# Turning the normalised memory by DMA instead of by TensorE

## The chip, the cores and the metric

The kernel runs on one core of a Trainium2 chip. The metric is the device time of one execution in microseconds (us). Below, PE is TensorE's matmul, PEld its weight load, DVE VectorE, ACT ScalarE, POOL GpSimd and SP SyncE, which issues the DMAs.

## The reference

Two layers work on `x` (512 tokens of 1024 numbers, float32). Each layer is a half-step SwiGLU block, a mixing block with three branches (stick-breaking attention, forgetting attention, attention over a memory), and another half-step SwiGLU block, each with an RMS norm before and after. What matters here is the memory branch: 256 memory rows, normalised once, give keys and values in both layers.

```python
def _rmsnorm(t, g):
    t32 = t.astype(jnp.float32)
    t32 = t32 * lax.rsqrt(jnp.mean(t32 * t32, axis=-1, keepdims=True) + RMS_EPS)
    return t32.astype(t.dtype) * g
...
    mem_n = _rmsnorm(mem, mem_norm_g)
...
        k_mem, v_mem = jnp.split(mem_n @ w_mem_kv[l], 2, axis=-1)
        o_mem = _memory_attention(_split_heads(q_mem, N_MEM_HEADS), _split_heads(k_mem, N_MEM_HEADS),
                                  _split_heads(v_mem, N_MEM_HEADS))
```

## The kernel before

**Products.** Every float32 product is made of three matmuls (`mm3`, lines 212 to 214): each operand is split into a high part and a low part, `h = round(v)` by ACT (line 182) and `l = v - h` by DVE (line 183), and `h*h`, `h*l` and `l*h` are summed in PSUM. A matmul contracts over the 128 partitions, so an operand must lie with the contracted dimension on the partitions.

**Queue.** The work is written as a list of jobs (`Queue`); a job has weight units and a generator that traces its matmuls. A `Unit` is loaded by SP into a raw buffer (`fetch`, line 256), split into `wh` and `wl` (four buffers each), and its raw buffer then takes the next unit. The planner that turns the trace into programs orders each engine's instructions ahead of the run, by the order in which they were traced and by when it reckons them ready; at run time every engine follows its own program and waits on semaphores. Tiles with one tag share a fixed number of buffers: "v" has six, "rs" one, "tri" two, "raw" two.

**Around the change.** The first feed-forward block of a layer ends in `down`: 144 matmuls of 128 x 512 in eight groups (`pda`), with three weight units for each of three passes. Between the first pass and the rest stands the job `mem_norm` (given as `aside`); in layer 0 the small vectors are turned (`vectors`) just ahead. As tokens finish, the chain of `Sub` (residual, norm, eight transposes `uta`, split into `us_a`) runs for the next block on ACT and DVE. After `down` come the jobs of `mem_kv`: `keys` (matmuls `pmk`, 128 x 256), `values` (`pmv`, 128 x 512), which contract over the 1024 numbers of a memory row and read `mn`, the memory turned so that those numbers lie on partitions. Then `q_mem` begins the mixing block, which needs all of `us_a`.

**`mem_norm` before.** Per layer it loads the two 128-row tiles of the memory (`mraw`, line 1062), multiplies each row with its own factor (`mem_rstd`, DVE, line 1063), and turns them with 16 transposes of 128 x 128 on PE (`mt`, line 1070), four to a PSUM bank. The norm's weight now runs along partitions, so ACT multiplies it in as a per-partition scale while it makes the high part (line 1075), and DVE makes the low part from the same bank (line 1076): eight of each per layer, 128 x 256. The weight itself, `memg`, is turned by PE in `vectors` (lines 122, 126, 128).

**A pattern that is there already.** A DMA transposes 16-bit words. The attention's stick heads and the feed-forward's hidden tiles turn 32-bit words by it: ACT copies the words so that all upper and all lower halves lie together (`turn_out`, line 1152; line 814), SP issues a transposing DMA (`turn_over`, line 1161; line 815), and ACT copies the halves back into words (line 1237; line 822).

Of the kernel before, what the change touches and what calls it, by code (L numbers as in the profile page):

```python
# [9 lines left out]
F32 = mybir.dt.float32  # L10
F32R = mybir.dt.float32r
BF16 = mybir.dt.bfloat16
U16 = mybir.dt.uint16
AF = mybir.ActivationFunctionType
ALU = mybir.AluOpType
# [3 lines left out]
P = 128  # L19
# [4 lines left out]
def kernel(  # L24
# [38 lines left out]
    nc = tc.nc  # L63
    _, S, D = x.shape
    M = mem.shape[1]
    L = w_in.shape[0]
    NT = S // P
    ND = D // P
    MT = M // P
# [12 lines left out]
    cst = ctx.enter_context(tc.tile_pool(name="cst", bufs=1))  # L82
# [6 lines left out]
    ident = cst.tile([P, P], F32, name="ident")  # L89
# [9 lines left out]
    def tmp(name):  # L99
        return sb.tile([P, S], F32, tag="f32t", bufs=8, name=name)  # L100
# [3 lines left out]
    def stile(shape, tag, name, dt=F32R):  # L104
        return sb.tile(shape, dt, tag=tag, bufs=BUFS[tag], name=name)
# [4 lines left out]
    def pbank(tag, name):  # L110
        return ps.tile([P, S], F32, tag=tag, bufs=4, name=name)

    gain_srcs = (ffn1_pre_g, ffn1_post_g, mix_pre_g, mix_post_g, ffn2_pre_g, ffn2_post_g)

    memg = cst.tile([P, ND], F32, name="memg")
    nbgate = cst.tile([P, L, 3 * ND], F32, name="nbgate")
    bgate = cst.tile([P, L, 3 * ND], F32, name="bgate")
    bfor = cst.tile([NH, L], F32, name="bfor")

    def vectors():  # L120
        vecs, n = tmp("vecs"), L * 3 * ND
        nc.gpsimd.dma_start(vecs[0:ND, 0:P], mem_norm_g.rearrange("(d p) -> d p", p=P))
        nc.gpsimd.dma_start(vecs[0:n, P:2 * P], b_gate.rearrange("l (d p) -> (l d) p", p=P))
        yield 0.0
        pt = pbank("z", "vecs_t")
        nc.tensor.transpose(pt[:, 0:ND], vecs[0:ND, 0:P], ident[0:ND, 0:ND])
        nc.tensor.transpose(pt[:, P:P + n], vecs[0:n, P:2 * P], ident[0:n, 0:n])
        nc.scalar.copy(memg[:], pt[:, 0:ND])
        nc.scalar.copy(bgate[:].rearrange("p l d -> p (l d)"), pt[:, P:P + n])
        nc.scalar.mul(nbgate[:].rearrange("p l d -> p (l d)"), pt[:, P:P + n], -1.0)  # L130
        yield 0.2
# [47 lines left out]
    def split(h_ap, l_ap, src, scale=None, later=False):  # L179

        if scale is None:
            both = [nc.scalar.copy(h_ap, src)]  # L182
            make = lambda: nc.vector.tensor_tensor(l_ap, src, h_ap.bitcast(F32), ALU.subtract)  # L183
        else:
            both = [nc.scalar.activation(h_ap, src, AF.Copy, scale=scale)]  # L185
            make = lambda: nc.vector.scalar_tensor_tensor(l_ap, src, scale, h_ap.bitcast(F32), ALU.mult, ALU.subtract)  # L186
        if later:
            return make
        both.append(make())
        if Q.pinned:  # L190
            for ins in both:
                tc.keep_in_program_order(ins)
        return both
# [292 lines left out]
    def rstd(st, a, b=None, beside=None):  # L486

        s, m, y, w = st[:, a:a + 1], st[:, 3:4], st[:, 4:5], st[:, 5:6]
        if b is None:
            nc.scalar.activation(y, s, AF.Ln, bias=eps_t[:])  # L490
            nc.vector.tensor_scalar(m, s, D * EPS, None, ALU.add)
        else:
            nc.vector.tensor_scalar(m, s, st[:, b:b + 1], D * EPS, ALU.add, ALU.add)
            nc.scalar.activation(y, m, AF.Ln)
            if beside is not None:
                beside()
        nc.scalar.activation(y, y, AF.Exp, scale=-0.5)

        nc.vector.scalar_tensor_tensor(w, m, y, y, ALU.mult, ALU.mult)
        nc.vector.scalar_tensor_tensor(y, w, -3.0, y, ALU.add, ALU.mult)  # L500
        return y

    class Sub:

# [61 lines left out]
        def residual(self, t):  # L566

            r = rstd(self.sf[t], 0, 1, self.held[t])
            f, h = self.fs[t], hT[t]
            if self.g_pre is None:  # L570
                for c in HF if t < NT - 1 else (HF[1], slice(0, S // 2), slice(S // 2, S)):
                    nc.vector.scalar_tensor_tensor(h[:, c], f[:, c], r, h[:, c], ALU.mult, ALU.add)
                    nc.sync.dma_start(out[0, t * P:(t + 1) * P, c], h[:, c])
            else:
                nc.vector.scalar_tensor_tensor(h[:], f[:], r, h[:], ALU.mult, ALU.add)
                self.squared(h[:], self.sh[t], 0, f[:])

        def normed(self, t, parts=(FULL_D,)):

            r = rstd(self.sh[t], 0)  # L580
            for c in parts:
                nc.vector.scalar_tensor_tensor(self.fs[t][:, c], hT[t][:, c], r, self.gq[:, c], ALU.mult, ALU.mult)
# [34 lines left out]
    def ffn(l, src, wg, wu, wd, dst, name, spare, parked, plan, aside=None):  # L617
# [348 lines left out]
        if name == "a0":  # L966
            Q.add([], vectors)
# [69 lines left out]
    mem_rstd = cst.tile([P, MT, 2], F32, name="mem_rstd")  # L1037
# [10 lines left out]
    def mem_norm(l, mn):  # L1048

        mn[:] = [stile([P, ND, M], "tri", f"mn{l}_{i}") for i in range(2)]  # L1050
        raws = []
        if l == 0:
            ms, r = mem_rstd[:, :, 0], mem_rstd[:, :, 1]
            for out_, in_, f, s in ((r, ms, AF.Ln, 1.0), (r, r, AF.Exp, -0.5)):
                tc.keep_in_program_order(nc.scalar.activation(out_, in_, f, scale=s))
            nc.vector.tensor_tensor(ms, ms, r, ALU.mult)
            nc.vector.tensor_tensor(ms, ms, r, ALU.mult)
            nc.vector.tensor_scalar(ms, ms, -0.5, 1.5, ALU.mult, ALU.add)
            nc.vector.tensor_tensor(r, r, ms, ALU.mult)
        for t in range(MT):  # L1060
            raw = stile([P, D], "v", f"mraw{l}_{t}", F32)
            nc.sync.dma_start(raw[:], mem[0, t * P:(t + 1) * P, :])
            nc.vector.tensor_scalar(raw[:], raw[:], mem_rstd[:, t, 1:2], None, ALU.mult)
            raws.append(raw)
        yield 0.0
        for i in range(ND // 2):
            pt = pbank("z", f"mt{l}_{i}")
            for j in range(2):
                for t in range(MT):
                    nc.tensor.transpose(pt[:, j * M + t * P:j * M + (t + 1) * P],  # L1070
                                        raws[t][:, (2 * i + j) * P:(2 * i + j + 1) * P], ident[:])
            for j in range(2):
                d = 2 * i + j
                src = pt[:, j * M:(j + 1) * M]
                nc.scalar.activation(mn[0][:, d], src, AF.Copy, scale=memg[:, d:d + 1])
                nc.vector.scalar_tensor_tensor(mn[1][:, d], src, memg[:, d:d + 1],
                                               mn[0][:, d].bitcast(F32), ALU.mult, ALU.subtract)
            yield 0.45

    def mem_kv(l, mn, ks, vs):  # L1080

# [551 lines left out]
    def begin():  # L1633
# [31 lines left out]
        def stats(t):  # L1665
            sub.squared(hT[t][:], sub.sh[t], 0, sub.fs[t][:])
            return rstd(sub.sh[t], 0)
# [59 lines left out]
    for l in LAYERS:  # L1727
        i, mn = 3 * l, []
        ma = ffn(l, subs[i], ffn1_w_gate, ffn1_w_up, ffn1_w_down, subs[i + 1], f"a{l}", "v",
                 park[2 * l] if l else None, PLAN, lambda l=l, mn=mn: mem_norm(l, mn))  # L1730
        rest = mem_kv(l, mn, *kvs[l])
        mb = mixing(l, subs[i + 1], *kvs[l], rest, subs[i + 2])
        if l == 0:
            Q.weave(begin(), ma["first"])
        else:
            for part, units in zip(mc["next"], (ma["early"][:2], ma["early"][2:])):
                part.extend(units)
            for un in ma["early"][2:]:
                un.place = "v"
            boundary(mc, mc["end"], ma["first"])  # L1740
        boundary(ma, ma["end"], mb["first"])
        mb["run"]()
        mc = ffn(l, subs[i + 2], ffn2_w_gate, ffn2_w_up, ffn2_w_down, subs[i + 3], f"c{l}", "o", park[2 * l + 1], PLAN)
        for part, units in zip(mb["next"], (mc["early"][:2], mc["early"][2:])):
                part.extend(units)
        boundary(mb, mb["end"], mc["first"])
# [25 lines left out]
```

## Time and profile before

| | us |
|---|---|
| median of 3 runs | 2338.09 |
| lowest, highest | 2337.59, 2340.59 |
| the profiled execution | 2342.67 |
| its span | 2340.9 |
| mean clock granted to PE | 0.999 |

The profile is of one execution. Its page lists each engine's busy time and share of the span. A line of the timeline gives start and duration in us, the engine, the line of the kernel, the operation, the tile written and those read, shapes and count, and in brackets how long the engine was idle before it and what released it. Matmuls overlap: the time that one takes from the engine is the distance between starts. A line of a tile's view gives a count, the shortest, median and longest duration in ns, the first and last start, and the shapes. A line of the windows view gives the stretch, its length, and the busy time and count of PE, PEld, DVE, ACT and POOL in it, then PE's clock, the DMA share and GB/s.

### The profile page before, as it was taken

How to read it: one execution, taken by the hardware profiler on the slowest of the kernel's cores; microseconds unless marked ns; L12 is line 12 of the kernel's file. 1: busy time of each engine (PE TensorE's matmuls, PEld its weight loads, DVE VectorE, ACT ScalarE, POOL GpSimd, SP SyncE). 2: the span in 40 equal slices, each digit the busy share in tenths (PEclk: the TensorE clock that was granted, in tenths of full speed). 3: DMA queues.
4: the chain of work that ended last, by engine and by line, in shares of the span. 5: the costliest groups of instructions: out<-in, count | busy, mean ns of one | idle time of the engine just before them, and what ended most of it. 6: DMA issues, size and time to landing. Idle time of an engine off the chain costs nothing.

```text
span 2340.9 us, 30650 instructions
## 1 busy us (share of the span) xinstructions
PE 2322.9 (99%) x11463; PEld 1960.2 (84%) x11463; DVE 1764.2 (75%) x2253; ACT 1509.8 (64%) x2216; POOL 81.2 (3%) x182
## 2 busy tenths in 40 slices
PE   9999999999999999999999999999999999999998
PEld 7888888888888888888898888888888888888887
DVE  8877877566777688878798788765677767887785
ACT  6677465577756556775656774655787674667744
POOL 0000000000111000000000000000001100000000
PEclk9999999999999999999999999999999999999999
DMA  6667454344423555674646665544444236466744
GB/s 207 190 176 221 146 189 141 93 115 114 122 73 105 187 186 164 185 199 152 226 144 186 196 185 179 185 114 95 119 105 116 81 118 200 160 195 176 220 138 144
DMA packets 340344, 365.44 MB, mean 156 GB/s; under 512 B 120778, under 2 KB 231650, under 8 KB 340196
## 3 DMA queue, kind: packets, MB, share of 16 engines
q1 hardware_dynamic: 340100, 363.46, 52.0%
q8 instruction: 90, 1.47, 0.3%
q14 instruction: 58, 0.48, 0.1%
q0 software_dynamic: 96, 0.03, 0.0%
HBM read 319.39 MB, written 16.78 MB: 144 GB/s over the span
## 4 chain that ended last, share of the span: by engine, by line
PE 85%; DMA 5%; ACT 4%; DVE 3%; issue 2%; DVEq 0%; SPq 0%; ACTq 0%
PE pg L213 4%; PE pg L212 4%; PE pg L214 4%; PE pda L213 3%; PE pda L212 3%; PE pda L214 3%; PE pdc L213 3%; PE pdc L212 3%; PE pdc L214 3%; PE pb L213 1%; PE pb L212 1%; PE pb L214 1%; PE pq L213 1%; PE pq L212 1%; PE pq L214 1%
## 5 line engine op out<-in xcount | busy, mean ns | idle before, releaser
L212 PE MATMUL pg<-us_a,wh_wg 128*128 128x512 f32 x384 | 150.4, 392 | 0.0
L213 PE MATMUL pg<-us_a,wh_wg 128*128 128x512 f32 x384 | 149.7, 390 | 0.0
L214 PE MATMUL pg<-us_a,wl_wg 128*128 128x512 f32 x384 | 149.6, 390 | 0.0
L183 DVE TENSOR_TENSOR wl_da<-raw_da,wh_da 128x1024 fp32r<-128x1024 f32 x50 | 60.8, 1223 | 44.6 <-ACT wh_da L182 44.4
L183 DVE TENSOR_TENSOR wl_dc<-raw_dc,wh_dc 128x1024 fp32r<-128x1024 f32 x50 | 61.0, 1223 | 44.1 <-ACT wh_dc L182 44.1
L213 PE MATMUL pdc<-wl_dc,ahc 128*128 128x512 f32 x224 | 87.7, 392 | 0.0
L213 PE MATMUL pda<-wl_da,aha 128*128 128x512 f32 x224 | 87.6, 391 | 0.0
L214 PE MATMUL pdc<-wh_dc,alc 128*128 128x512 f32 x224 | 87.2, 389 | 0.0
L214 PE MATMUL pda<-wh_da,ala 128*128 128x512 f32 x224 | 87.2, 389 | 0.0
L212 PE MATMUL pdc<-wh_dc,ahc 128*128 128x512 f32 x224 | 86.6, 390 | 0.5 <-ACT pdc L895 0.5
L212 PE MATMUL pda<-wh_da,aha 128*128 128x512 f32 x224 | 86.5, 389 | 0.0
L186 DVE SCALAR_TENSOR_TENSOR wl_wg<-raw_wg,wh_wg 128x1024 fp32r<-128x1024 f32 x48 | 58.7, 1223 | 35.8 <-ACT wh_wg L185 35.6
L214 PEld LDWEIGHTS pg<-us_a,wl_wg 128*128 128x128 f32 x384 | 72.1, 188 | 15.1
L212 PEld LDWEIGHTS pg<-us_a,wh_wg 128*128 128x128 f32 x384 | 72.1, 188 | 14.2
L213 PEld LDWEIGHTS pg<-us_a,wh_wg 128*128 128x128 f32 x384 | 72.1, 188 | 14.2
L182 ACT CAST wh_da<-raw_da 128x1024 fp32r<-128x1024 f32 x50 | 52.1, 1050 | 46.9 <-PE pda L214 19.4
L182 ACT CAST wh_dc<-raw_dc 128x1024 fp32r<-128x1024 f32 x50 | 52.3, 1049 | 46.0 <-DMA raw_dc<-in_ffn_w_down_dram 13.9
L182 ACT CAST wh_uc<-raw_uc 128x1024 fp32r<-128x1024 f32 x44 | 46.4, 1054 | 34.5 <-PE pwc1g L214 7.7
L182 ACT CAST wh_ua<-raw_ua 128x1024 fp32r<-128x1024 f32 x44 | 46.2, 1052 | 30.2 <-PE pwa0g L214 7.6
L183 DVE TENSOR_TENSOR wl_uc<-raw_uc,wh_uc 128x1024 fp32r<-128x1024 f32 x44 | 53.7, 1220 | 14.5 <-ACT wh_uc L182 14.5
L183 DVE TENSOR_TENSOR wl_gc<-raw_gc,wh_gc 128x1024 fp32r<-128x1024 f32 x40 | 48.5, 1221 | 20.3 <-ACT wh_gc L182 20.3
L1237 ACT COPY pws<-ts 128x1024 uint16<-128x1024 uint16 (+1 forms) x64 | 55.4, 914 | 12.2 <-DMA ts<-ns 11.9
(643 smaller groups left out, 7921.1 us busy)
## 6 DMA issues: line engine op xcount, KB each, us to landing
raw_da<-in_ffn_w_down_dram SPq DMA_DIRECT2D x66, 512.0 KB, 5.3
raw_dc<-in_ffn_w_down_dram SPq DMA_DIRECT2D x66, 512.0 KB, 4.6
raw_ga<-in_ffn_w_gate_dram SPq DMA_DIRECT2D x52, 512.0 KB, 4.7
raw_ua<-in_ffn_w_up_dram SPq DMA_DIRECT2D x52, 512.0 KB, 4.5
raw_gc<-in_ffn_w_gate_dram SPq DMA_DIRECT2D x52, 512.0 KB, 4.1
raw_uc<-in_ffn_w_up_dram SPq DMA_DIRECT2D x52, 512.0 KB, 4.4
raw_wg<-in_w_gate_dram SPq DMA_DIRECT2D x48, 512.0 KB, 3.6
raw_wo<-in_w_out_dram SPq DMA_DIRECT2D x24, 512.0 KB, 3.7
```

Of the source, the lines that this page charges most:

```text
L182: both = [nc.scalar.copy(h_ap, src)]
L183: make = lambda: nc.vector.tensor_tensor(l_ap, src, h_ap.bitcast(F32), ALU.subtract)
L186: make = lambda: nc.vector.scalar_tensor_tensor(l_ap, src, scale, h_ap.bitcast(F32), ALU.mult, ALU.subtract)
L212: nc.tensor.matmul(pt, lh, rh, start=start, stop=False, skip_group_check=free)
L213: nc.tensor.matmul(pt, lh, rl, start=False, stop=False, skip_group_check=free)
L214: nc.tensor.matmul(pt, ll, rh, start=False, stop=stop, skip_group_check=free)
L1237: nc.scalar.copy(block_words(word, i), over[:, :, c:c + i + 1])
```

## The change

The 16 PE transposes per layer go, with the eight high and eight low parts that read them from PSUM, and the turned weight `memg`. Instead the weight is loaded as a row into all 128 partitions (`grow`, tag "rs", once per layer), and DVE multiplies a tile by its rows' factors and by that row in one operation. Then `flip_out` has ACT copy the tile's halves apart into a second "v" tile and SP issue one transposing DMA of all 2048 half-words per partition back into the first; `flip_back` has ACT put the words together, and `split` makes one high and one low part of 128 x 1024 per tile.

```diff
-    memg = cst.tile([P, ND], F32, name="memg")
...
-        nc.gpsimd.dma_start(vecs[0:ND, 0:P], mem_norm_g.rearrange("(d p) -> d p", p=P))
...
-        nc.tensor.transpose(pt[:, 0:ND], vecs[0:ND, 0:P], ident[0:ND, 0:ND])
...
-        nc.scalar.copy(memg[:], pt[:, 0:ND])
...
+    def flip_out(words, halves):
+
+        nc.scalar.copy(halves.bitcast(U16).rearrange("p (h k) -> p h k", h=2), words.bitcast(U16).rearrange("p (k h) -> p h k", h=2))
+        nc.sync.dma_start_transpose(words.bitcast(U16).rearrange("p (r q) -> p r q", q=P), halves.bitcast(U16))
+
+    def flip_back(words, over):
+
+        nc.scalar.copy(words.bitcast(U16).rearrange("p (k h) -> p h k", h=2), over.bitcast(U16).rearrange("p (h k) -> p h k", h=2))
...
     def mem_norm(l, mn):
 
         mn[:] = [stile([P, ND, M], "tri", f"mn{l}_{i}") for i in range(2)]
-        raws = []
+        raws, grow = [], stile([P, D], "rs", f"mg{l}", F32)
+        nc.sync.dma_start(grow[:], mem_norm_g.rearrange("(a d) -> a d", a=1).broadcast_to([P, D]))
...
-            nc.vector.tensor_scalar(raw[:], raw[:], mem_rstd[:, t, 1:2], None, ALU.mult)
+            nc.vector.scalar_tensor_tensor(raw[:], raw[:], mem_rstd[:, t, 1:2], grow[:], ALU.mult, ALU.mult)
             raws.append(raw)
         yield 0.0
-        for i in range(ND // 2):
-            pt = pbank("z", f"mt{l}_{i}")
-            for j in range(2):
-                for t in range(MT):
-                    nc.tensor.transpose(pt[:, j * M + t * P:j * M + (t + 1) * P],
-                                        raws[t][:, (2 * i + j) * P:(2 * i + j + 1) * P], ident[:])
-            for j in range(2):
-                d = 2 * i + j
-                src = pt[:, j * M:(j + 1) * M]
-                nc.scalar.activation(mn[0][:, d], src, AF.Copy, scale=memg[:, d:d + 1])
-                nc.vector.scalar_tensor_tensor(mn[1][:, d], src, memg[:, d:d + 1],
-                                               mn[0][:, d].bitcast(F32), ALU.mult, ALU.subtract)
-            yield 0.45
+        turned = []
+        for t, raw in enumerate(raws):
+            halves = stile([P, D], "v", f"mh{l}_{t}", F32)
+            flip_out(raw[:], halves[:])
+            turned.append(halves)
+            yield 0.0
+        for t, (raw, halves) in enumerate(zip(raws, turned)):
+            flip_back(halves[:], raw[:])
+            c = slice(t * P, (t + 1) * P)
+            split(mn[0][:, :, c], mn[1][:, :, c], halves[:].rearrange("p (d q) -> p d q", q=P))
+            yield 0.0
```

## The prediction

> **What bounds the kernel.** I read the page's busy times first, then the windows view of the two stretches that the change touches, then the timeline of PE inside them.
>
> ```profile
> PE 2322.9 (99%) x11463; PEld 1960.2 (84%) x11463; DVE 1764.2 (75%) x2253; ACT 1509.8 (64%) x2216; POOL 81.2 (3%) x182
> ```
> ```profile
> 326.10:348.65 22.55, 22.01 (x110) 18.21 (x109) 20.85 (x40) 17.00 (x42) 0.00 (x0) 1.00 0.22 84
> 1481.60:1509.48 27.88, 27.50 (x133) 22.79 (x134) 23.77 (x42) 19.11 (x45) 0.00 (x0) 1.00 0.32 113
> ```
>
> PE is idle for 18 us of 2340.9, so whatever leaves PE comes off the end, and whatever makes PE wait is added to it. The two windows run from the first scaling of a memory tile to the first key matmul that reads `mn`, once per layer; the columns are length, then busy us of PE, PEld, DVE, ACT and POOL, PE's clock, DMA share and GB/s. DVE (20.85 of 22.55) and ACT (17.00 of 22.55) have little room in layer 0, more in layer 1. So the question is what PE gains, and whether ACT and DVE still deliver in time.
>
> **What leaves PE.** Layer 0, then layer 1, in PE's timeline (start, duration, instruction):
>
> ```profile
> 325.97 0.39 PE L212 MATMUL pda<-wh_da,hida 128*128 128x512 f32 x1
> 326.88 2.19 PE L1070 MATMUL mt<-ident,mraw 128*128 128x128 f32 x16 [0.53 <-DVE mraw L1063]
> 328.83 0.48 PE L213 MATMUL pda<-wl_da,hida 128*128 128x512 f32 x1
> 329.14 0.40 PE L214 MATMUL pda<-wh_da,hida 128*128 128x512 f32 x1
> ```
> ```profile
> 1480.95 0.39 PE L214 MATMUL pda<-wh_da,hida 128*128 128x512 f32 x1
> 1481.61 0.66 PE L1070 MATMUL mt<-ident,mraw 128*128 128x128 f32 x4 [0.28 <-DVE mraw L1063]
> 1482.02 0.47 PE L212 MATMUL pda<-wh_da,hida 128*128 128x512 f32 x1
> ...
> 1484.87 0.39 PE L212 MATMUL pda<-wh_da,hida 128*128 128x512 f32 x1
> ...
> 1486.23 0.39 PE L212 MATMUL pda<-wh_da,hida 128*128 128x512 f32 x1
> 1486.99 1.53 PE L1070 MATMUL mt<-ident,mraw 128*128 128x128 f32 x12 [0.37 <-DVE mraw L1063]
> 1488.27 0.47 PE L213 MATMUL pda<-wl_da,hida 128*128 128x512 f32 x1
> ```
>
> Matmuls overlap, so I count starts, not durations. Undisturbed they start every 1.36/6 = 0.227 us (1484.87 to 1486.23 is six). Layer 0: 328.83 - 325.97 - 0.227 = 2.63, and the next start comes 0.31 behind instead of 0.227: with 0.03 for the starts after it, 2.74 us go. Layer 1: (1.07 - 0.227) + (2.04 - 0.227) = 2.65, and about 0.1 for each restart: 2.86.
>
> The transpose of `mem_norm_g` goes too; its neighbour for the gate's bias stays:
>
> ```profile
> 311.89 0.22 PE L126 MATMUL vecs_t<-ident,vecs 8*128 8x8 f32 x1
> 312.05 0.26 PE L127 MATMUL vecs_t<-ident,vecs 48*128 48x48 f32 x1
> ```
>
> That is 0.16 us from start to start. All of it: 2.74 + 2.86 + 0.16 = **5.76 us, the most that the change can bring**.
>
> **What ACT and DVE get.** The same kind of copies and transposes exist in the stick heads (`turn_out`, `turn_over`), which gives their prices; the rows are count, ns min/median/max, first and last start, forms.
>
> ```profile
> L1237 ACT COPY pws<-ts x64: 467/910/1370, 446.6 to 1781.4; 128x1024 uint16<-128x1024 uint16 x16, 128x768 uint16<-128x768 uint16 x16, 128x512 uint16<-128x512 uint16 x16, 128x256 uint16<-128x256 uint16 x16
> ...
> L1152 ACT COPY ns<-ts x48: 812/833/1065, 440.6 to 1775.7; 128x768 uint16<-128x768 uint16 x32, 128x1024 uint16<-128x1024 uint16 x16
> L1161 SPq DMA_TRANSPOSE ts<-ns x48: 1209/1232/2306, 441.9 to 1776.6; - x48
> ```
> ```profile
> L1075 ACT ACTIVATE mn<-mt,memg x16: 465/482/509, 328.1 to 1491.4; 128x256 fp32r<-128x256 f32 x16
> L1076 DVE SCALAR_TENSOR_TENSOR mn<-mt,memg,mn x16: 473/476/485, 328.6 to 1492.9; 128x256 fp32r<-128x256 f32 x16
> ```
> ```profile
> L1063 DVE TENSOR_SCALAR mraw<-mraw,mem_rstd x4: 745/747/752, 326.1 to 1486.2; 128x1024 f32<-128x1024 f32 x4
> ```
> ```profile
> L582 DVE SCALAR_TENSOR_TENSOR fa<-hfa,nha,gqa x8: 1276/1278/1285, 339.4 to 1521.6; 128x1024 f32<-128x1024 f32 x8
> ```
> ```profile
> L182 ACT CAST wh_mk<-raw_mk x8: 1032/1054/1057, 340.0 to 1514.3; 128x1024 fp32r<-128x1024 f32 x8
> L183 DVE TENSOR_TENSOR wl_mk<-raw_mk,wh_mk x8: 1215/1218/1226, 341.2 to 1516.5; 128x1024 fp32r<-128x1024 f32 x8
> ```
>
> `flip_back` writes 2048 half-words with a stride: the L1237 copy grows from 0.47 us (256) to 1.37 (1024), 0.30 per 256, so 1.37 + 4 x 0.30 = 2.57. `flip_out` reads with a stride: L1152 grows by about 0.22 from 768 to 1024, 1.05 + 4 x 0.22 = 1.93. Per layer ACT gets two of each and two casts of 1.05, 11.1 us, and loses eight of 0.48, 3.86: **+7.2 us**. DVE: each scaling grows from 0.75 to 1.28 (the form of L582), the eight 0.476 become two of 1.22: 1.06 - 1.37 = -0.3 us.
>
> Layer 0: the window shrinks to 22.55 - 2.74 = 19.8 us, in which ACT would have 17.00 + 7.2 = 24.2 us of work and DVE 20.5. ACT is **4.4 us over**, DVE 0.7. Layer 1: 26.3 us for ACT in 25.0, 1.3 over. In the other direction nothing is won: PE has no idle time left to lose.
>
> What absorbs the lateness is the lead that ACT and DVE have over PE. The tightest in layer 0 is the second key-weight unit:
>
> ```profile
> 346.97 2.35 DVE L183 TENSOR_TENSOR wl_mk<-raw_mk,wh_mk 128x1024 fp32r<-128x1024 f32 x2
> ```
> ```profile
> L212 PE MATMUL pmk<-mn,wh_mk x64: 278/283/365, 348.6 to 1521.6; 128*128 128x256 f32 x64
> ```
> ```profile
> L212 PE MATMUL pmk<-mn,wh_mk x32: 278/283/365, 1509.5 to 1521.6; 128*128 128x256 f32 x32
> ```
>
> (The key matmuls begin at 348.6 in layer 0 and 1509.5 in layer 1.) Its low part is there at 346.97 + 1.18 = 348.15. PE wants it 14 half-width matmuls after the first, at about half the pitch of 0.227 (an estimate from the rows above): 350.2. Its cast can start only when PE leaves an earlier unit's buffer, so it moves with PE and keeps 2.1 us of lead. I take 4.4 - 2.1 = **2.3 us of PE waiting in layer 0**, bounds 0 (the late work is all from the residual chains, which nobody needs yet) and 4.4 (none is covered). Layer 1: 1.3 is under the lead there, 0; upper bound 1.3.
>
> [...]
>
> **When PE comes early.** In layer 1 the third unit of `down`'s second weight set is bound by its load:
>
> ```profile
> 1482.22 2.00 ACT L182 CAST wh_da<-raw_da 128x1024 fp32r<-128x1024 f32 x2 [0.83 <-DVE fa L549]
> ```
> ```profile
> 1480.81 0.75 DVE L1063 TENSOR_SCALAR mraw<-mraw,mem_rstd 128x1024 f32<-128x1024 f32 x1
> 1481.47 0.68 DVE L549 SCALAR_TENSOR_TENSOR fa<-pda,gpa 128x512 f32<-128x512 f32 x1
> 1483.31 2.36 DVE L183 TENSOR_TENSOR wl_da<-raw_da,wh_da 128x1024 fp32r<-128x1024 f32 x2 [1.15 <-ACT wh_da L182]
> ```
>
> Its low part is done at 1483.31 + 1.18 = 1484.49 and PE wants it one matmul after 1484.87, 1485.10. Without the first four transposes PE is there 0.94 earlier, 1484.16: 0.3 us of wait.
>
> **What else is issued.** SP gets four transposes and two loads of the weight row. The transposes are twice the size of L1161's, so I take 2 x 1.23 = 2.46 us of issue each, and for landing
>
> ```profile
> DMA to landing us min/median/max: 3.0/3.5/8.1
> ```
>
> (the 64 transposes of 256 KB in the feed-forward part, line 815) 2.46 + (3.5 - 1.23) = 4.7 us, between 3.0 and 16.2 (twice 8.1). Behind their waits on SP stand loads of key weights and saves of `h`, none wanted before 340; DMA is busy 22% and 32% in these windows. Layer 0: scaling 326.1 to 327.4, `flip_out` to 329.3 and 331.2, second transpose issued at 331.8, landed 336.5 (the first 334.0; between 331.2 and then ACT has the residual chain, and what is queued behind a `flip_back` that still waits are weight casts, squares and copies into PE's banks), `flip_back`, cast and low part 2.57 + 1.05 + 1.22 = 4.84 more: `mn` is whole at 341.3, wanted at 348.6 - 2.9 = 345.7. The weight row takes the "rs" buffer when the last turned plane leaves it:
>
> ```profile
> L1222 DVE TENSOR_TENSOR_SCAN ns<-ns,cut x48: 921/955/1539, 437.4 to 1773.6; 128x383 f32<-128x383 f32 x32, 128x511 f32<-128x511 f32 x16
> ...
> L1194 POOL MEMSET cut<- x2: 634/636/637, 206.4 to 1369.1; 128x640 f32 x2
> ```
>
> `cut` took it at 206.4; now the weight row does and `cut` waits until 329, still 100 us before its first reader. A wait for that buffer on SP would hold weight loads: 0, at most 1 us. The "v" buffers (six) hold three weight units, two raw tiles and now two turned ones; the seventh is free once the pair at 1483.31 ends, ahead of the second `flip_out`: 0. The four PSUM banks that `mt` leaves had no one waiting.
>
> **Sum**: -5.76 + 2.3 + 0.3 = -3.2 us. The profiled execution took 2342.7 (span 2340.9 and 1.8 around it), 4.6 over the median 2338.09; -3.2 makes 2339.5 of it and **2334.9** of the median. About 0.2% (4.7 us) is what a measurement of this kernel can tell from no change.
>
> **Rivals.**
> 1. *ACT's lead covers everything.* Only the 0.3 stays: 2332.6. For it: much of what ACT does there is squares and residual chains. Against it: ACT and DVE both over.
> 2. *`flip_out` gets in front of that cast in layer 1.* Its input is ready at 1480.81 + 1.28 = 1482.1, the cast starts at 1482.22. Then the low part is late by 1.93 more: 2336.8. The order is fixed ahead of the run, and the cast was traced first, so it is the less likely.
> 3. *The expected gain is eaten by the weight pipeline*: all of ACT's 4.4 and 1.3 reach PE: -5.76 + 5.7 + 0.3, 2338.3.
> 4. *The transposes land late, slower than before.* ACT stands at `flip_back`, and weight casts behind it. With landing time L, `mn` is whole at 336.6 + L in layer 0 (decides from L = 9.1) and at 1487.5 + 1.93 + L + 4.84 = 1494.3 + L in layer 1 (PE there at 1509.5 - 2.9; L = 12.3). At L = 16.2 PE waits 7.1 + 3.9 = 11.0: +5.2, 2343.3. Against it: 3.5 is the median and DMA is quiet.
> 5. *PE's clock drops after such a wait.* If all of ACT's 4.4 us reach PE in one piece in layer 0 and PE then runs as long at half its clock, 4.4 us of matmuls cost 4.4 more: -5.76 + 8.8 + 0.3, 2341.4. Against it: the windows show the clock at 1.00; but the longest idle time in them is 0.53 us, so they cannot show it. [...]
>
> **Chances.** Forecast 0.44, its own range 2333.0 to 2337.0; rival 1 0.22; 2 0.09; 3 0.11; 4 0.10; 5 0.04. Faster by over 0.2% (under 2333.4): rival 1 and a fifth of the forecast, 0.31. Slower by over 0.2%: rival 4 and a little of 3 and 5, 0.12. Within: 0.57. The range goes from rival 1, less 1 us of scatter, to between rivals 3 and 4: 2331.5 to 2341.5.
>
> **What would show it.** PE rows with `mt` gone and `pda` starts 0.227 apart through 326 to 329; `flip_back` near 2.6 us, transposes landing near 4.7; a PE wait of about 2 us near 344 to 352 for `wl_mk` or `mn`, next to none at 1505 to 1520. Wrong would be: no such wait (rival 1), one of over 5 us (rival 4), or PE waits far from both windows, which nothing here foresees.

## The result, and the profile after

| | us |
|---|---|
| before, median of 6 runs | 2338.50 (2337.39 to 2341.13) |
| after, median of 6 runs | 2346.05 (2344.57 to 2348.77) |
| ratio, 95% interval | 1.0033 (1.0020 to 1.0046) |
| profiled execution before: span | 2340.9 |
| profiled execution after: span | 2344.3 |

The changed kernel is slower by 7.6 us (4.7 to 10.8 by the interval). The forecast of 2334.9 and its range to 2341.5 were wrong. The two profiled executions lie only 3.4 us apart, because the one shown of before lies 4 us above the median of its kind.

The page of the changed kernel gives the busy times:

```profile
PE 2321.8 (99%) x11430; PEld 1957.7 (84%) x11430; DVE 1762.4 (75%) x2241; ACT 1521.2 (65%) x2211; POOL 78.6 (3%) x181
```

PE has 33 instructions less on record and is still busy for nearly as long; ACT has gained 11.4 us. The view of PE's waits (line and tile that waited, who ended it, then total us, times and the longest) says where the loss is:

```profile
PE pmk L208 <- DVE nha L496: 4.8, 1, 4.8
PE pda L208 <- ACT pda L849: 2.2, 1, 2.2
...
PE uta L597 <- DVE fa L587: 0.6, 1, 0.6
```

Before, no wait of PE exceeded 1.2 us. The first and the third are in layer 0, the second in layer 1. (Lines of the changed kernel stand a few off those before: `mm3` is 208 to 210, `split`'s cast and low part 178 and 179, the square of a result 549, its scaling 554, the copy into a bank 849.)

PE's timeline around the first:

```profile
339.89 0.39 PE L210 MATMUL pda<-wh_da,hida 128*128 128x512 f32 x1
345.10 0.55 PE L208 MATMUL pmk<-mn,wh_mk 128*128 128x256 f32 x1 [4.82 <-DVE nha L496]
...
346.31 0.41 PE L210 MATMUL pmk<-mn,wl_mk 128*128 128x256 f32 x1
346.52 0.63 PE L208 MATMUL pda<-wh_da,hida 128*128 128x512 f32 x1
346.94 0.63 PE L209 MATMUL pda<-wl_da,hida 128*128 128x512 f32 x1
```

Until 339.89 `pda` matmuls start 0.227 apart. After the wait the key matmuls (`pmk`), half as wide, start 0.21 apart (0.12 before) and the `pda` matmuls 0.43: PE runs at half its clock (0.50 from 342.79 to 349.62, in the last section). That this is the clock, and not a late operand, is seen in the windows (columns as in the prediction; the clock is the third number from the end):

```profile
326.08:340.00 13.92, 13.92 (x63) 11.44 (x61) 7.67 (x11) 13.55 (x14) 1.17 (x3) 1.00 0.50 113
340.00:345.00 5.00, 0.28 (x2) 0.00 (x0) 4.75 (x10) 5.00 (x14) 0.00 (x0) 0.78 0.35 105
345.00:350.00 5.00, 4.90 (x15) 4.19 (x16) 4.20 (x10) 2.40 (x8) 0.00 (x0) 0.54 0.26 105
```

While PE stands still, ACT is busy for 5.00 of 5.00 us; DVE, idle for much of the time before, for 4.75. What PE waits for is not `mn`: that is whole at 342.6 (below). It is a bank of PSUM, the memory in which PE's sums stand. The releasers that the profile names are no operands of the key matmul: `nha L496` on DVE is a 128x1 factor that comes right behind a scaling of line 554 and ends within 0.1 us of it, and the weight load of the same matmul had waited 5.2 us for the square of line 549 on ACT. A finished group of `pda` keeps its bank until ACT has squared it (line 549) and DVE has scaled it (line 554), and ACT then copies the old sums into a free bank (line 849) before PE can start the next group. ACT's timeline:

```profile
332.48 2.53 ACT L506 COPY mh<-mraw 128x2048 uint16<-128x2048 uint16 x1 [0.37 <-DMA mraw<-mh]
...
336.76 2.52 ACT L506 COPY mh<-mraw 128x2048 uint16<-128x2048 uint16 x1
339.14 1.04 ACT L178 CAST wh_mk<-raw_mk 128x1024 fp32r<-128x1024 f32 x1
340.09 1.04 ACT L178 CAST mn<-mh 128x1024 fp32r<-128x1024 f32 x1
...
342.17 0.57 ACT L549 ACTIVATE sqa<-pda 128x512 f32<-128x512 f32 x1
...
345.31 0.58 ACT L849 COPY pda<-fa 128x512 f32<-128x512 f32 x1
```

and DVE's, where the scaling stands behind work that had waited for ACT:

```profile
341.36 1.22 DVE L179 TENSOR_TENSOR mn<-mh,mn 128x1024 fp32r<-128x1024 f32 x1
...
344.27 0.68 DVE L554 SCALAR_TENSOR_TENSOR fa<-pda,gpa 128x512 f32<-128x512 f32 x1
```

Read backwards: PE starts at 345.10, behind the scaling that ends at 344.95. In DVE's order that scaling stood behind low parts and residual work, the first of which had waited 1.91 us for a cast on ACT, until 340.22. The bank needs the square of the same group too (by the order of the groups, the one at 342.17). In ACT's order it stood behind both `flip_back`, two casts of `mn`, two weight casts and the square of a residual. The copy into the bank of the last group was issued at 345.31. In the kernel before, the same two stood at

```profile
335.50 0.58 ACT L844 COPY pda<-fa 128x512 f32<-128x512 f32 x1
...
339.40 0.58 ACT L544 ACTIVATE sqa<-pda 128x512 f32<-128x512 f32 x1
```

The copy is now 9.8 us later and the square 2.8, although PE ends the third late group 3.6 us earlier than before (339.89 against 343.45).

Layer 1 has the same chain, shorter; there the first `flip_back` also kept ACT idle for 1.10 us until its transpose had landed. ACT's timeline:

```profile
1500.12 2.53 ACT L506 COPY mh<-mraw 128x2048 uint16<-128x2048 uint16 x1
...
1505.34 0.61 ACT L549 ACTIVATE sqa<-pda 128x512 f32<-128x512 f32 x1
...
1507.84 0.59 ACT L849 COPY pda<-fa 128x512 f32<-128x512 f32 x1
```

and PE's, which goes on when that copy is done:

```profile
1505.90 0.39 PE L210 MATMUL pda<-wh_da,hida 128*128 128x512 f32 x1
1508.48 0.50 PE L208 MATMUL pda<-wh_da,hida 128*128 128x512 f32 x1 [2.19 <-ACT pda L849]
```

The new operations themselves, in the view of the tile `mh` (count, ns min/median/max, first and last start):

```profile
L501 ACT COPY mh<-mraw x4: 1889/1900/1902, 326.1 to 1490.6; 128x2048 uint16<-128x2048 uint16 x4
L502 SPq DMA_TRANSPOSE mraw<-mh x4: 1526/1858/2502, 328.0 to 1492.5; - x4
L506 ACT COPY mh<-mraw x4: 2515/2523/2527, 332.5 to 1500.1; 128x2048 uint16<-128x2048 uint16 x4
...
DMA to landing us min/median/max: 4.4/4.8/5.2
```

So each piece costs what was forecast (1.93, 2.57 and 4.7 us); what they displace was not seen.

**Theory A:** the regrouping copies and casts fill ACT, and what frees the PSUM banks stands behind them; PE waits for a bank, and in layer 0 the wait also costs it the clock. **Rivals:** the row weight costs (E), the transposes come late (B), much of the loss lies elsewhere (D), the matmuls behind the wait are slow for another reason than the clock (F).

### The profile page after: what moved, and what is told of

Read it like the earlier page. It is cut to its first block, busy times and chain, and to the rows that moved or that the text cites. A ratio compares the mean times of both kernels' runs of the same rounds, so it can differ in the third digit from the quotient of the medians.

```text
span 2344.3 us, 30567 instructions
## 1 busy us (share of the span) xinstructions
PE 2321.8 (99%) x11430; PEld 1957.7 (84%) x11430; DVE 1762.4 (75%) x2241; ACT 1521.2 (65%) x2211; POOL 78.6 (3%) x181
## 4 chain that ended last, share of the span: by engine, by line
PE 82%; DMA 6%; ACT 5%; DVE 4%; issue 3%; SPq 0%; DVEq 0%; ACTq 0%
PE pg L208 4%; PE pg L209 4%; PE pg L210 4%; PE pdc L209 3%; PE pdc L210 3%; PE pdc L208 3%; PE pda L209 2%; PE pda L208 2%; PE pda L210 2%; PE pb L208 1%; PE pb L209 1%; PE pb L210 1%; PE pq L208 1%; PE pq L209 1%; PE pk L208 1%
## 5 line engine op out<-in xcount | busy, mean ns | idle before, releaser
L179 DVE TENSOR_TENSOR wl_ga<-raw_ga,wh_ga 128x1024 fp32r<-128x1024 f32 x40 | 48.5, 1220 | 19.8 <-ACT wh_ga L178 19.8
```

## The experiments

Ratios are against the kernel before, run beside each group; 0.001 is 2.3 us.

### Parts of the change alone

The first keeps PE's transposes and takes only the row weight; the next two turn by DMA in one layer and on PE in the other.

```diff
-        turned = []
-        for t, raw in enumerate(raws):
...
+        for i in range(ND // 2):
+            pt = pbank("z", f"mt{l}_{i}")
...
+            for j in range(2):
+                d = 2 * i + j
+                split(mn[0][:, d], mn[1][:, d], pt[:, j * M:(j + 1) * M])
+            yield 0.45
```

> Only the first part of the change: the norm's weight is multiplied in by rows (the loaded weight row, one DVE operation per tile) and its turned copy is gone, but PE still turns the tiles and ACT and DVE make eight high and eight low parts per layer from the banks, without a scale. Theory A (the time is lost on ACT: the regrouping copies and the casts of mn stand ahead of the squares that free PSUM banks): this part is free, 2338.3, within 1 us of before, no PE wait above 1.3 us in either window. Rival E (the weight row, its load or its longer DVE operation costs the time): 2341 or more, with PE waiting for mraw at the transposes for over 1.3 us.

> The row weight in both layers, the DMA transposes in layer 0 alone; layer 1 turns on PE. Theory A: layer 0 keeps its 4.8 us wait for a bank at 345, its 6.8 us of half clock (2.2 us more on the matmuls inside) and the 0.75 us wait for fa near 370, against 2.7 saved: +5 us, 2343.5. Rival D (a large part of the 7.6 us lies in neither window): under +3, 2341 or less, although the waits are there.

> The row weight in both layers, the DMA transposes in layer 1 alone. Theory A: the waits of 0.5 us (low part of the last weight set) and 2.4 us (bank) and some 0.3 us of restarts against 2.9 saved: +0.3, 2338.8, and the clock stays at 1.00 because no wait reaches 3 us. Rival D: layer 1 costs 2 us or more, 2340.5 and above, since the two layers must make up 7.6 us together.

| | median us | ratio (95%) |
|---|---|---|
| row weight only | 2338.31 | 0.9995 (0.9986 to 1.0004) |
| DMA in layer 0 only | 2343.79 | 1.0020 (1.0011 to 1.0029) |
| DMA in layer 1 only | 2337.89 | 0.9994 (0.9985 to 1.0003) |

The row weight costs nothing: E falls. Layer 0 costs 5.8 us over the row weight alone (0.0025), near the 5 expected; layer 1 costs nothing that can be told. In layer 0 the wait is the same again, in PE's timeline of the kernel with DMA in layer 0 (an execution 4.2 us above its median):

```profile
346.17 0.55 PE L208 MATMUL pmk<-mn,wh_mk 128*128 128x256 f32 x1 [4.88 <-DVE nha L496]
```

In layer 1 alone the bank's wait is there, 1.97 us, and one expectation failed: the clock did drop behind it, to 0.50 from 1499.34 to 1502.75, and in PE's timeline of the kernel with DMA in layer 1 the matmuls start 0.43 apart.

```profile
1499.27 0.76 PE L208 MATMUL pda<-wh_da,hida 128*128 128x512 f32 x1 [1.97 <-ACT pda L849]
1499.83 0.63 PE L209 MATMUL pda<-wl_da,hida 128*128 128x512 f32 x1
1500.26 0.63 PE L210 MATMUL pda<-wh_da,hida 128*128 128x512 f32 x1
```

No run shows the bound of 3 us by which the clock was to stay at 1.00: this wait of 1.97 us was enough, and the one of 2.19 us in layer 1 of the changed kernel left it at 1.00.

The two layers and the row weight add up to 4.4 us by their ratios, the whole change to 7.6; the intervals overlap. D falls for the larger part, but up to 3 us of the loss are not assigned.

### The join traced last

`flip_back` and the split become a job of their own just ahead of the keys, so that the planner ranks the residual work of `down` before them.

```diff
+    def mem_join(mn):
+        for t, (raw, halves) in enumerate(flipped):
             flip_back(halves[:], raw[:])
...
     def mem_kv(l, mn, ks, vs):
...
+        Q.add([], lambda: mem_join(mn))
         for c in range(2):
```

> The changed kernel with flip_back and the split of the turned tiles traced after the late groups of down, just ahead of the keys, so that the copies into the banks and the squares stand earlier in ACT's order. Theory A: no wait for a bank above 1 us in either layer, no half clock; mn comes later, so PE waits up to 2 us for it at the keys: 2333 to 2337. Rival B (mn comes late whatever the order, because the transposes land late or the queue is behind): the wait only moves to the keys and stays near 5 us, 2342 or more.

2349.89 us, 1.0042 (1.0030 to 1.0055): the slowest of all, and a miss for A's number. PE's timeline of layer 0 tells why:

```profile
345.93 1.04 PE L597 MATMUL uta<-ident,fa 128*128 128x128 f32 x8
350.04 0.62 PE L208 MATMUL pmk<-mn,wh_mk 128*128 128x256 f32 x3 [3.07 <-ACT mn L178]
```

The wait for a bank inside `down` is gone: PE runs through to 347.0. But in layer 0 `mn` is now what is late, because the second `flip_back` stands behind the squares: the key matmuls wait 3.1 us for it and then 1.9 for a bank. In layer 1 they wait 4.1 us for a bank. The mean granted clock of the profiled execution is 0.997, against 0.999 before: over its 2349.7 us some 12 to 16 us at half clock, an estimate from these numbers. So A's expectation of no long bank wait and no half clock failed; what holds is that the order of the same work moves the wait, and this order does not give both in time (other orders were not run). The number is that of rival B, but in layer 0 neither `flip_back` was waiting for its DMA.

### The clock alone

Twenty matmuls that nobody reads keep PE busy in the gap of layer 0.

```diff
+    FILL = 20
...
+        def fill():
+            src, pt = tmp("fill")[:].bitcast(BF16), pbank("z", "fill")
+            nc.gpsimd.memset(src, 0.0)
+            for _ in range(FILL):
+                nc.tensor.matmul(pt[:], src[:, 0:P], src[:, 0:S], start=True, stop=True)
...
+            if name == "da0" and t == 2:
+                fill()
```

> The changed kernel with 20 more matmuls (16-bit, 128x512, on a zeroed tile, their result used by nobody) on PE in layer 0 between the third late group and the keys, where PE stands still for 4.8 us. Theory A with the clock: at 512 columns they keep PE busy for about 4 to 4.5 us of the wait, the first key matmul still waits for its bank until 345.1, no stretch of half clock follows, key and down matmuls behind it start 0.12 and 0.227 apart, and 2.2 us come back: about 2343.9. Rival F (the matmuls behind the wait are slow for another reason, such as a late operand): the same spacing of 0.21 and 0.43 and 2346.

PE's timeline in layer 0, with the twenty in one row:

```profile
341.09 4.49 PE L1011 MATMUL fill<-fill 128*128 128x512 bf16 x20
346.73 0.50 PE L209 MATMUL pda<-wh_da,hida 128*128 128x512 f32 x1 [1.15 <-ACT pda L850]
347.06 0.40 PE L210 MATMUL pda<-wl_da,hida 128*128 128x512 f32 x1
347.30 0.39 PE L211 MATMUL pda<-wh_da,hida 128*128 128x512 f32 x1
```

PE is still held until ACT's copy into the bank, now at the last group instead of the keys (the six key matmuls moved behind it in the planned order), but the matmuls behind it start 0.23 to 0.24 apart again, where the changed kernel had 0.43: rival F falls, the half clock came from PE standing still. The time, 2345.34 us, 1.0023 (1.0014 to 1.0032), is lower than that of the changed kernel by 2.3 us in the ratio, the amount expected, though the intervals overlap; the six matmuls that no longer fit ahead of the copy may give some of it back, and the profiled execution has 3.41 us of half clock in layer 1 (1508.54 to 1511.95, granted 0.50) that the one of the changed kernel does not have.

### Less work on ACT

`flip_back` is given to POOL, to DVE, or one tile each to ACT and DVE. The transposes and their order on SP stay.

```diff
-        nc.scalar.copy(words.bitcast(U16).rearrange("p (k h) -> p h k", h=2), over.bitcast(U16).rearrange("p (h k) -> p h k", h=2))
+        nc.gpsimd.tensor_copy(words.bitcast(U16).rearrange("p (k h) -> p h k", h=2), over.bitcast(U16).rearrange("p (h k) -> p h k", h=2))
```

In the second kernel `nc.vector.tensor_copy` stands there; the third passes the copy as an argument:

```diff
-            flip_back(halves[:], raw[:])
+            flip_back(halves[:], raw[:], nc.vector.tensor_copy if t else nc.scalar.copy)
```

> The changed kernel with flip_back on POOL, which is idle there: ACT loses 2 x 2.52 us per layer. No row shows POOL with 2048 half-words; its memset of 640 words takes 0.64 us, so I take 2 to 4 us for one copy. Theory A: up to 4 us, mn is whole by 342 and the squares stand at their old place: waits for a bank under 1 us in both layers, no half clock, 2333 to 2336. If a copy takes over 5 us, the casts of mn, which stand ahead of the squares in ACT's order, hold ACT and the wait for the bank comes back, 2340 or more. Rival B (the transposes are what is late): no change against the changed kernel, 2346.

> The changed kernel with flip_back on DVE. Theory A (the pair of ACT and DVE is full in layer 0: 24.2 and 20.5 us of work in 19.8): ACT loses 5 us and DVE gets two copies of 1 to 2.5 us; DVE's scaling that frees the banks and its low parts then come late in layer 0, a wait of 1 to 4 us, and layer 1, where DVE stands idle for 1490 to 1500, has none: 2334 to 2341. Rival G (only ACT's order matters, DVE has room): no wait in either layer, 2333.

> The changed kernel with flip_back of the first tile on ACT (2.52 us) and of the second on DVE (1.35 us): ACT is relieved of 2.5 us per layer instead of 5.0, DVE gets 1.35 instead of 2.7. Theory A (a balance of ACT and DVE): between the two kernels; the squares and the scaling come about 2.5 us earlier than in the changed kernel, so the wait for a bank in layer 0 falls from 4.8 to about 2.3, which is too short for half clock, and layer 1 has none over 0.5: 2337 to 2340. Rival J (any flip_back on ACT ahead of the squares costs the whole wait): 2343 or more.

| `flip_back` on | median us | ratio (95%) |
|---|---|---|
| ACT (the change) | 2346.05 | 1.0033 (1.0020 to 1.0046) |
| POOL | 2347.35 | 1.0035 (1.0021 to 1.0048) |
| DVE | 2338.16 | 0.9999 (0.9990 to 1.0008) |
| ACT and DVE | 2338.14 | 0.9994 (0.9985 to 1.0003) |

DVE needs only 1.35 us for the copy that takes ACT 2.52, in the view of its tile:

```profile
L506 DVE COPY mh<-mraw x4: 1342/1346/1348, 332.4 to 1495.1; 128x2048 uint16<-128x2048 uint16 x4
```

The whole loss goes away with the same transposes, landing as before (median 4.6 us): B falls, and A stands. Rival G, no wait at all, falls too. What is left in layer 0 with DVE are, in the view of PE's waits, some for DVE's residual chain (and 0.3 for a bank),

```profile
PE pmv L208 <- DVE nha L495: 1.7, 1, 1.7
PE uta L597 <- DVE fa L587: 1.0, 1, 1.0
```

and with one tile on each engine (the same window, 320 to 385)

```profile
PE pmk L208 <- DVE fa L554: 1.0, 1, 1.0
PE pmv L208 <- DVE nha L495: 0.4, 1, 0.4
PE uta L597 <- DVE nha L495: 0.3, 1, 0.3
```

2.5 us off ACT took 3.8 us off the wait for a bank (4.8 to 1.0), more than the 2.5 expected, and rival J falls. That 2.3 us are too short for half clock was not shown: with DMA in layer 1 alone 1.97 us were enough. Neither version gains what PE was spared, 2.7 and 2.9 us: the waits listed around both layers' `down` and keys add up to 3.7 us with DVE and 3.1 with both. The rest of the saving is not found, but the intervals reach 2 us to either side.

POOL was a failure of its own kind. The time is that of rival B, but no wait of PE for a bank is left around `down`, as A says. Its copies took 2.52 to 3.47 us, within the expected range. DVE's timeline beside them:

```profile
331.35 0.68 DVE L554 SCALAR_TENSOR_TENSOR fa<-pda,gpa 128x512 f32<-128x512 f32 x1
...
333.34 3.49 DVE L179 TENSOR_TENSOR wl_da<-raw_da,wh_da 128x1024 fp32r<-128x1024 f32 x1
336.76 2.40 DVE L495 SCALAR_TENSOR_TENSOR nfa<-nfa 128x1 f32<-128x1 f32 x1
```

and POOL's, busy in one piece from 333.24:

```profile
333.24 5.95 POOL L506 COPY mh<-mraw 128x2048 uint16<-128x2048 uint16 x2 [4.04 <-DMA mraw<-mh]
```

A low part that takes 1.22 us elsewhere took 3.49, and a factor of 0.21 us took 2.40. The factor ends together with POOL's second copy, at 339.2; the low part ends at 336.8, 1.0 us behind the first copy. PE then waited for DVE (5.4 us for `fa` over both layers). Idle POOL was no free engine here.

### Not doing the work twice

The normalised memory is the same in both layers. Layer 0 stores both parts of `mn`, layer 1 loads them; layer 0 makes them on PE, by DMA with `flip_back` on DVE, or by DMA with one tile on each.

```diff
+    mnsave = nc.dram_tensor("mnsave", (2, P, ND * M), F32, kind="Internal").ap()
...
+        flat = lambda i: mn[i][:].rearrange("p d m -> p (d m)").bitcast(F32)
+        if l > 0:
+            for i in range(2):
+                nc.sync.dma_start(flat(i), mnsave[i])
+            return
...
+        for i in range(2):
+            nc.sync.dma_start(mnsave[i], flat(i))
```

> The memory's normalised parts are the same in both layers. Layer 0 makes them as in the row-weight kernel (transposes on PE), stores both parts to DRAM, and layer 1 loads them instead of turning anything: 2 MB more written, 2 MB read, 1 MB of raw memory and the weight row not read. Theory A (what decides is the work on ACT and DVE ahead of the squares, PE's share is only 2.9 us per layer): layer 1 loses PE's 2.9 us, four DVE and sixteen ACT and DVE operations, and waits for nothing: 2338.3 - 2.9 = 2335.4. Rival H (the two loads of 1 MB come late or push weight loads back): PE waits at the keys of layer 1 or for a weight unit near 1480 to 1510 for 2 us or more, 2337.5 and above.

> Layer 0 as in the kernel with flip_back on DVE, both parts stored, layer 1 loads them. Theory A: layer 0 keeps that kernel's 3.5 us of waits (DVE's normed rows and the factor for them come late), layer 1 drops its two waits of 0.5 us: 2338.2 - 1.0 = 2337.2; in layer 0 the waits stand at the same places within 0.5 us. Rival I (the waits of layer 0 hang on something else than DVE, such as the queue of loads): they change by over 1 us with the stores.

> Layer 0 turns by DMA with one flip_back on ACT and one on DVE, stores both parts, and layer 1 loads them. Theory A: layer 0 keeps the 2.3 us of waits of the kernel with both engines against 2.7 saved on PE, layer 1 saves 2.9 and waits for nothing: 2338.3 - 0.4 - 2.9 = 2335.0, some 0.4 us beside the kernel that keeps PE's transposes in layer 0, which this measurement can't tell apart. Rival K (the stores add to layer 0's waits, since the DMA way leaves ACT and DVE no room there): 2337.5 or more.

| layer 0 | median us | ratio (95%) |
|---|---|---|
| on PE | 2336.45 | 0.9983 (0.9974 to 0.9992) |
| by DMA, DVE | 2338.02 | 0.9991 (0.9982 to 1.0000) |
| by DMA, both | 2337.24 | 0.9990 (0.9981 to 0.9999) |

The first is faster than both kernels, by 4.0 us against before (1.9 to 6.1), and 2.8 us in the ratio below the row weight alone, where 2.9 leave PE in layer 1; the intervals of these two overlap. Its two loads are issued long ahead, in the view of the tile `mn`,

```profile
L1060 SPq DMA_DIRECT2D mn<-mnsave x2: 339/339/339, 1428.9 to 1455.8; - x2
```

and the view lists no wait of PE between 1440 and 1560: rival H falls. In the second, layer 0's waits stand where they did, 1.8 and 1.0 us (rival I falls). The third missed A's 2335.0 by 2.2 us and comes close to K's 2337.5. Its wait for a bank came to 1.4 instead of 1.0 us and that of `pmv` to 0.9 instead of 0.4; the stores may have a part in it (K), but 0.9 us in one execution doesn't settle that. With DMA in layer 0 nothing is won over PE there.

## Why the prediction was wrong, point by point

- **What leaves PE, 5.76 us: right as far as it was tested.** The transposes are gone, `pda` starts stand 0.227 apart, and layer 1 gives 2.8 of its 2.86 us once nothing waits there (layer 1 loaded from DRAM), a difference about as large as its noise. The row weight costs nothing that can be told, as costed.
- **The prices of the new operations: right.** 1.90, 2.52, 4.8 us against 1.93, 2.57, 4.7. No wait of PE in layer 0 names a buffer of SBUF or a load, and `mn` was whole at 341.36 + 1.22 = 342.6 (341.3 forecast).
- **The load, "ACT is 4.4 us over": near in size, in part by luck.** PE waited 4.82 us in one piece in layer 0. But the square came 2.8 us late and the copy 9.8, 2.5 us less work on ACT took 3.8 us off the wait, and in layer 1, where the sum said 1.3, it was 2.19.
- **The step that failed: "What absorbs the lateness is the lead that ACT and DVE have over PE. The tightest in layer 0 is the second key-weight unit".** The lead was looked for in weights and in `mn`, the operands PE reads next. The tightest consumer was the PSUM bank: square, scaling, copy. The lower bound of that step takes the late work for residual chains, "which nobody needs yet"; the part on what else is issued even lists "weight casts, squares and copies into PE's banks" behind `flip_back`, and did not follow the squares and copies to PE. So the 2.1 us of lead absorbed nothing, and 2.3 was under half of what came (4.82 + 0.6).
- **"Layer 1: 1.3 is under the lead there, 0": failed by the same step.** It was 2.19 us for a bank and 0.32 for a low part. The 0.3 us foreseen at the third unit of `down`'s second weight set did not show there. A balance of work over a window says how much is late, not which piece; in layer 1 ACT was busy for 14.31 of the 15.50 us from 1493.00, although the sum had it only slightly over.
- **The clock: a rival's mechanism, given too small a chance.** Rival 5 stood at 0.04 and as an alternative to rival 3; but it followed both times that more than 4.4 us reached PE in one piece in layer 0: with 4.82 us the clock was 0.50 for 6.83 us from the middle of the wait, and after the 4.88 us with DMA in layer 0 alone `pda` matmuls start 0.43 apart. By an estimate it costs 2.2 us here (half of the 4.52 us of busy PE inside the half-clock stretch), not 4.4.
- **The sum by what was measured**: -5.8 from PE; layer 0 +4.8 +0.6 +2.2 and 0.3 for the restart; layer 1 +2.2 +0.3 and 0.3 for restarts: +4.9. The 0.3 is an estimate from the starts around the wait in layer 1: 1505.90 to 1509.06 is 3.16 us, less three pitches of 0.227 and the wait of 2.19. The measured 7.6 (4.7 to 10.8) holds it at its lower end. What may add to it is a half-clock stretch in layer 1 in other executions, 1.7 us each (half of 3.41 us of busy PE, an estimate), as the kernels with DMA in layer 1 alone and with the filler have it. This is argued and not shown for the changed kernel: the mean clocks of its six executions do differ, 0.996 to 0.998, but the fastest is one of the two at 0.996.

## What to carry to other kernels

When work is moved to an engine that is far from the bound on average, list what stands behind it in that engine's order and follow each piece to what it frees as well as to what it feeds: here a square whose result nobody reads soon was among what released a PSUM bank. Price a wait of the matmul engine with the clock it costs afterwards (here 0.50 for 6.83 us with a wait of 4.82 us). And before a step is made cheaper, see whether it has to be done twice: that paid where moving it to other engines did not.

## What the hardware showed that was not expected

In these profiles PE's clock changes stretch by stretch, on a fixed grid. The changed kernel has half clock for 6.83 us from 342.79, which is two times 3.413, and again from 2343.00 to the end of the run, 586 times 3.413 us behind the first. Windows cut on that grid show what comes before a drop; the number after the length is PE's busy time. The changed kernel:

```profile
339.38:342.79 3.41, 0.90 (x4) 0.40 (x3) 2.57 (x5) 3.41 (x8) 0.00 (x0) 1.00 0.07 8
342.79:349.62 6.83, 4.52 (x14) 3.88 (x15) 6.38 (x14) 4.23 (x15) 0.00 (x0) 0.50 0.41 149
...
1506.73:1510.14 3.41, 1.66 (x7) 1.40 (x8) 3.41 (x10) 2.23 (x9) 0.00 (x0) 1.00 0.46 122
1510.14:1513.56 3.42, 3.42 (x20) 2.92 (x20) 3.35 (x6) 3.39 (x7) 0.00 (x0) 1.00 0.49 185
```

and the kernel with `mn` kept and `flip_back` on DVE:

```profile
358.42:361.83 3.41, 1.56 (x13) 1.39 (x12) 2.80 (x7) 2.46 (x4) 0.00 (x0) 1.00 0.76 288
361.83:365.24 3.41, 3.41 (x9) 2.66 (x9) 2.94 (x6) 1.47 (x5) 0.00 (x0) 0.50 0.64 167
```

PE busy for 1.66 us of a grid stretch: full clock next. Busy for 1.56: half clock next. From 10 us after the start to 15 us before the end, in the kernel before and in the changed one, each grid stretch at full clock with PE busy for 1.66 us or more was followed by full clock, and so was one with 1.67 us in the kernel with `flip_back` on DVE. Behind stretches with 0.90 us (the changed kernel), 1.32 (the filler), 1.44 (DMA in layer 1 alone), 1.49 (`mn` kept, layer 0 on PE) and the 1.56 above the clock was 0.50; the line lies between 1.56 and 1.66, near half the stretch. At the end of the run it does not hold: the changed kernel has full clock behind one with 1.54. So busy time alone is not the whole rule. Between the ends, a wait of 1.97 us cost the clock in one kernel (it fell into a single stretch, 1495.93 to 1499.34) and one of 2.19 us didn't in another (it was cut in two at 1506.73). Where the grid falls differs between the profiles: counted back by 3.413 us from these two, its first line is 0.9 us behind the span's start in the one and 1.5 in the other. So the same wait may cost 1.7 us more (the estimate above) or not.
